# Up projection of a gated feed-forward layer: eight pairs of column tiles computed as seven block products, in an interleaved order

## The chip, the cores and the metric

The kernel runs on one core of a Trainium2 chip. The metric is the device time of one execution in microseconds, the median of several runs; smaller is better. Inputs are laid out by the host (slices, transposes, stacks), and everything that is arithmetic runs on the chip.

## The reference, cut to what matters

One layer of a hybrid trunk for 512 tokens with 1024 channels, in float32. A convolution branch and a linear-attention branch are merged and added to x, giving `h`; then comes the feed-forward part that the change is in (F = 2816):

```python
u2 = _rmsnorm(h, norm2_g[l])
z = _causal_dwconv(u2 @ w_ffn_up[l], ffn_dw_w[l], ffn_dw_b[l])
h = h + (jax.nn.silu(z[..., :FFN_DIM]) * z[..., FFN_DIM:]) @ w_ffn_down[l]
return _rmsnorm(h, final_g)
```

The up projection has 5632 columns, of which column c and column 2816 + c form one product (value and gate). The convolution runs over time, is causal, 3 wide, and separate for each column.

## The kernel before, in words

**Precision.** Each float32 operand is held as a sum of two numbers in a shorter format, hi and lo, and each product is three matmuls (`mm3`, L306 to L311: lo x hi, hi x lo, hi x hi). Of a weight block the hi part is a cast on ScalarE and the lo part a subtraction on VectorE (`split_weight`, L266 and L267; for the blocks of the down projection L239 and L240).

**Weights.** A list `order` names every weight block in the order of its use. `load` lets SyncE's queue (SP) fetch the next block, 128 x 1024 numbers or 512 KB, into a ring of 4 raw places; `split_weight` splits the next one and calls `load`; `weight` hands out a split block after `prefetch` has had the next LOOK = 2 split. So a load's place in SP's queue follows from the split before it, and a load waits until the last reader of its raw place is done. Each engine runs its instructions in the order in which the program issues them.

**The up projection.** A column tile is 128 of the 5632 columns for all 512 tokens, in one PSUM bank. `col_tile` (L313) goes over the 8 blocks of 128 channels, 3 matmuls of 128 x 512 each: 24. There are FT = 22 value tiles i and 22 gate tiles FT + i. On a finished tile `ffn_conv` (L1099) runs the convolution: a ScalarE operation with the bias (L1102) and two VectorE operations (L1104), both reading PSUM. `glu` applies silu to the value tile (L1110) and multiplies it by the gate tile (L1112).

**Pairs and groups.** The 22 products are taken in pairs (p, q), eleven in all, and the pairs in GROUPS of 4, 3 and 4. `first_of_pair` and `second_of_pair` (L1121, L1129) form sums and differences of the halves of 256 tokens and split them into hi and lo (`fsplit`, L1116 to L1118). After a group's pairs, `seven("w_down", ...)` (L972) multiplies them by the rows of the down projection and adds into `hres` (L1023). It computes each 2 x 2 block product (two halves of tokens, the two members of a pair) by seven block products in place of eight, named a11, a12, s1, n2, s4, n3, a22, from sums of the activations and sums of the weights. GpSimd's DMA queue adds weight blocks up while loading (L208, L225). The same function did the projection `w_o` before.

**The order around the change.** Group 0's first pair is done in a loop of its own (L1212 to L1218): its first three tiles go by halves of 256 tokens, since the last tokens are not normalized yet. From then on each pair is four whole tiles in the order p, FT + p, q, FT + q, then first and second of pair; at the end of a group the down projection follows, and then the next group's first tile. The working tiles `w`, `f`, `v` have two buffers each, `kept` (summed down-projection weights) two, `tmp` five; PSUM has five `mm` and three `ax` banks.

## Time and profile before

| what | value |
|---|---|
| median of 3 runs | 837.06 us (836.98 to 837.22) |
| the profiled execution | 838.15 us |
| its span in the trace | 836.5 us |
| granted TensorE clock | 0.998 |
| feed-forward part in the trace | about 482 to 836.5 us |
| HBM read, written | 95.03 MB, 2.10 MB |

The profiled execution is one run by itself; the span is the time between its first and last instruction in the trace. All rows shown from the trace are of this execution. PE is TensorE's matmul, PEld its weight load, DVE VectorE, ACT ScalarE, POOL GpSimd, SP SyncE. A row like `wlo<-raw,whi 128x1024 fp32r<-128x1024 f32 x42 | 50.9, 1216 | 3.5` means: output and inputs by the program's names, shape and type, 42 of them, 50.9 us busy together, 1216 ns each on average, 3.5 us idle of that engine just before them. A window row gives for each engine the busy time and in brackets the number of instructions in it. Matmuls overlap one another, so their durations do not add up; the distance of their starts does.

### The profile page before, as it was taken

Reading aid. Unit: us, or ns where it says so; the run is one execution under the profiler, and the core shown is the slowest. Engines: PE = TensorE matmul, PEld = TensorE weight load, DVE = VectorE, ACT = ScalarE, POOL = GpSimd, SP = SyncE. Lnnn points to the kernel's source line nnn. Section 1 sums busy time; section 2 is a strip of 40 time slices with the busy share of each in tenths; the row PEclk is TensorE's granted clock in tenths of the full one; section 3 lists DMA queues with packets and bytes.
Section 4 is the critical chain, followed back from the end, with each engine's and each line's share of the span. In section 5 each row is a group of like instructions: output and inputs, shape, how many; then the busy total and the mean of one; then the engine's idle time right before and its main releaser. Section 6 shows DMA issues by size and latency. Waiting matters only on the chain.

```text
span 836.5 us, 9981 instructions
## 1 busy us (share of the span) xinstructions
PE 827.9 (99%) x3821; PEld 692.4 (83%) x3821; DVE 651.6 (78%) x927; ACT 392.0 (47%) x544; POOL 43.1 (5%) x65
## 2 busy tenths in 40 slices
PE   9999999999999999999999999999999999999996
PEld 8888888888888888888888898888888888888885
DVE  5689879999998798744688858778757687677795
ACT  6723337537533422449435554444434444444454
POOL 1000000000001100000001000001000010000111
PEclk9999999999999999999999999999999999999999
DMA  8233222222322322222348643234742249222462
GB/s 313 99 103 101 85 100 88 93 98 76 101 76 76 126 92 88 98 100 77 102 100 229 194 157 108 94 97 105 214 151 88 66 88 284 101 87 93 101 125 102
DMA packets 28305, 97.79 MB, mean 117 GB/s; under 512 B 3208, under 2 KB 3344, under 8 KB 28256
## 3 DMA queue, kind: packets, MB, share of 16 engines
q1 hardware_dynamic: 24800, 85.35, 29.8%
q0 software_dynamic: 3456, 11.80, 8.3%
q8 instruction: 30, 0.49, 0.2%
q14 instruction: 19, 0.16, 0.1%
HBM read 95.03 MB, written 2.10 MB: 116 GB/s over the span
## 4 chain that ended last, share of the span: by engine, by line
PE 97%; DVE 1%; DMA 0%; issue 0%; ACT 0%; POOL 0%; POOLq 0%; SPq 0%; ACTq 0%
PE mm L309 29%; PE mm L311 29%; PE mm L310 29%; PE mm L521 3%; PE ax L862 1%; PE ax L309 1%; PE ax L311 1%; PE ax L310 1%; PE ax L435 1%; PE ax L864 1%; PE ax L844 1%; PE ax L831 0%; DVE hres L1023 0%; DMA x<-in_x_dram 0%; PE ax L830 0%; PE ax L388 0%
## 5 line engine op out<-in xcount | busy, mean ns | idle before, releaser
L309 PE MATMUL mm<-uh,wlo 128*128 128x512 f32 (+1 forms) x760 | 293.0, 385 | 0.0
L311 PE MATMUL mm<-uh,whi 128*128 128x512 f32 (+1 forms) x760 | 290.8, 383 | 0.0
L310 PE MATMUL mm<-ul,whi 128*128 128x512 f32 (+1 forms) x760 | 290.6, 382 | 0.0
L266 ACT CAST whi<-raw 128x1024 fp32r<-128x1024 f32 x114 | 118.8, 1046 | 124.3 <-PE mm L311 92.4
L267 DVE TENSOR_TENSOR wlo<-raw,whi 128x1024 fp32r<-128x1024 f32 x114 | 138.4, 1218 | 36.1 <-ACT whi L266 35.9
L311 PEld LDWEIGHTS mm<-uh,whi 128*128 128x128 f32 x760 | 142.8, 188 | 28.0
L310 PEld LDWEIGHTS mm<-ul,whi 128*128 128x128 f32 x760 | 142.9, 188 | 27.8
L309 PEld LDWEIGHTS mm<-uh,wlo 128*128 128x128 f32 x760 | 142.9, 188 | 27.2
L615 DVE SCALAR_TENSOR_TENSOR c<-h,pp,c 128x511 f32<-128x511 f32 (+14 forms) x240 | 162.4, 727 | 0.7
L1104 DVE SCALAR_TENSOR_TENSOR tmp<-mm,pp,tmp 128x511 f32<-128x511 f32 x88 | 65.9, 749 | 68.7 <-ACT tmp L1102 67.5
L1102 ACT ACTIVATE tmp<-mm,pp 128x512 f32<-128x512 f32 x44 | 34.3, 780 | 61.8 <-PE mm L311 61.8
L239 ACT CAST whi<-kept 128x1024 fp32r<-128x1024 f32 (+1 forms) x32 | 31.7, 995 | 23.1 <-PE mm L311 14.4
L240 DVE TENSOR_TENSOR wlo<-kept,whi 128x1024 fp32r<-128x1024 f32 (+1 forms) x32 | 36.6, 1152 | 3.0 <-ACT whi L239 2.8
L1023 DVE TENSOR_TENSOR hres<-hres,mm 128x512 f32<-128x512 f32 (+1 forms) x49 | 32.7, 671 | 3.4 <-PE mm L311 2.8
L239 ACT CAST whi<-raw 128x1024 fp32r<-128x1024 f32 (+1 forms) x24 | 23.7, 995 | 19.1 <-PE mm L311 19.0
L240 DVE TENSOR_TENSOR wlo<-raw,whi 128x1024 fp32r<-128x1024 f32 (+1 forms) x24 | 27.3, 1152 | 3.4 <-ACT whi L239 3.3
L310 PE MATMUL mm<-wlo,sh 128*128 128x512 f32 x66 | 25.8, 391 | 0.0
L311 PE MATMUL mm<-whi,sh 128*128 128x512 f32 x66 | 25.7, 390 | 0.0
L309 PE MATMUL mm<-whi,sl 128*128 128x512 f32 x66 | 25.5, 389 | 0.0
L309 PE MATMUL mm<-h,wlo 128*128 128x512 f32 x64 | 25.0, 391 | 0.0
L310 PE MATMUL mm<-h,whi 128*128 128x512 f32 x64 | 24.9, 389 | 0.0
L311 PE MATMUL mm<-h,whi 128*128 128x512 f32 x64 | 24.9, 389 | 0.0
(258 smaller groups left out, 1131.6 us busy)
## 6 DMA issues: line engine op xcount, KB each, us to landing
raw<-in_w_up_dram SPq DMA_DIRECT2D x44, 512.0 KB, 3.4
raw<-in_w_glu_dram SPq DMA_DIRECT2D x16, 512.0 KB, 3.4
raw<-in_w_down_dram SPq DMA_DIRECT2D x15, 512.0 KB, 3.3
kept<-in_w_down_dram POOLq DMA_DIRECT2D x10, 512.0 KB, 5.4
raw<-in_w_v_dram SPq DMA_DIRECT2D x8, 512.0 KB, 3.9
raw<-in_w_qk_dram SPq DMA_DIRECT2D x8, 512.0 KB, 3.2
raw<-in_w_r_dram SPq DMA_DIRECT2D x8, 512.0 KB, 3.3
raw<-in_w_gb_dram SPq DMA_DIRECT2D x8, 512.0 KB, 3.2
```

Of the source, the lines that this page charges most:

```text
L239: nc.scalar.copy(hi, raw)
L240: nc.vector.tensor_tensor(lo, raw, hi.bitcast(F32), ALU.subtract)
L266: nc.scalar.copy(hi, raw)
L267: pace[0] = nc.vector.tensor_tensor(lo, raw, hi.bitcast(F32), ALU.subtract)
L309: nc.tensor.matmul(acc, ll, rh, start=first, stop=False, **kw)
L310: nc.tensor.matmul(acc, lh, rl, start=False, stop=False, **kw)
L311: nc.tensor.matmul(acc, lh, rh, start=False, stop=last, **kw)
L521: nc.tensor.matmul(acc, act, ready[k // 2][wi][:, j], start=first, stop=last)
L615: nc.vector.scalar_tensor_tensor(y[:, s:], c[:, : T - s], w, y[:, s:], ALU.mult, ALU.add)
L1023: nc.vector.tensor_tensor(hres[t, n][:, c], hres[t, n][:, c], acc[:, c], op)
L1102: nc.scalar.activation(z, acc, AF.Identity, bias=pp[:, PP_FB + m : PP_FB + m + 1], scale=w[2])
L1104: nc.vector.scalar_tensor_tensor(z[:, s:], acc[:, : T - s], w[j], z[:, s:], ALU.mult, ALU.add)
```

## The change

In 8 of the 11 pairs (two of group 0, three of group 1, three of group 2) the second member q is computed as one 2 x 2 block product: two halves of 256 tokens by the two column tiles q and FT + q, over two halves of 512 channels. `up_pair` does it by seven block products of 4 channel blocks, 3 matmuls each, 256 tokens wide: 84 matmuls of 128 x 256 in place of 48 of 128 x 512.

- **Weights.** The two raw blocks and a third raw place for sums form four parts, x1, x3, x2, x4, split in this order (1024, 1024, 1024 and 512 columns). `up_sums` adds the blocks' halves on GpSimd: three additions of 128 x 512 after the split of x1, one after the split of x3.
- **Activations.** `sum_acts` forms, once, in group 0, the four sums s1, n2, s4, n3 of the halves of `u2` (10 VectorE operations of 128 x 1024) and splits them into hi and lo. They lie in buffers that were free or are shared (`kept`, `x`, `gain`, `btmp`, `us`).
- **Results.** The products are put together in two working tiles c1, c2: 4 copies from PSUM on ScalarE and 3 VectorE operations of 256 columns, and the convolution of q's tiles reads these. It read PSUM before.
- **Order.** `up_plan` writes the sequence. A unit is one seven-product pair and the two plain tiles of the next first member f, cut at k blocks and interleaved with the parts. So plain tiles run one place ahead; the last unit of a group computes the first member of the next group ahead of the down projection ("closes"), and the first unit of the groups opens differently ("opens").
- **Refill.** `refill` replaces the single `load` after each split: 4 raw entries ahead of the splits, and 2 in the up projection from group 0's seven-product part on.
- **Small moves.** `att` and `gate_up` lie in another pool; the load of `final_g` moves from the start of the feed-forward part to just before the last down projection; the down projection's loads are kept in program order; `w`, `f` and `v` have one buffer each; silu, gate and product are separate functions.

The core of the diff, first the order, the weights and the tiles (a line of "..." marks what is left out):

```diff
+        pairs = GROUPS[gi]
+        whole = range(KT)
+        def halves(*cuts):
+            return [range(a, b) for a, b in zip((0, *cuts), (*cuts, KT))]
+        def unit(q, f, kind):
+            a, b = f, FT + f
+            x1, x3, x2, x4 = (("part", q, part) for part in ("x1", "x3", "x2", "x4"))
+            a1, a2 = (("tile", a, ks) for ks in halves(4))
+            if kind == "opens":
+                b1, b2, b3 = (("tile", b, ks) for ks in halves(4, 6))
+                seq = [a1, x1, a2, x3, b1, x2, b2, x4, ("second", q), b3]
+            elif kind == "closes":
+                a1, a2, a3 = (("tile", a, ks) for ks in halves(3, 6))
+                seq = [x1, a1, x3, a2, x2, a3, x4, ("second", q), ("tile", b, whole)]
+            else:
+                b1, b2 = (("tile", b, ks) for ks in halves(4))
+                seq = [x1, a1, x3, a2, x2, b1, x4, ("second", q), b2]
+            return seq + [("first", f)]
+        firsts = [p for p, _ in pairs[1:]]
+        if gi + 1 < len(GROUPS):
+            firsts.append(GROUPS[gi + 1][0][0])
+        plan = []
+        n = 0
+        if gi == 0:
+            (p, q), (f, _) = pairs[1:3]
+            for i, role in ((p, "first"), (q, "second"), (f, "first")):
+                plan += [("tile", i, whole), ("tile", FT + i, whole), (role, i)]
+            n = 2
+        while n < len(firsts):
+            last = n + 1 == len(firsts) and gi + 1 < len(GROUPS)
+            kind = "closes" if last else "opens" if n == 0 else ""
+            plan += unit(pairs[n][1], firsts[n], kind)
+            n += 1
+        if n < len(pairs):
+            q = pairs[n][1]
+            plan += [("tile", q, whole), ("tile", FT + q, whole), ("second", q)]
+        return plan
+    def up_order(plan):
+        out = []
+        for what, i, *rest in plan:
+            if what == "part":
+                out.append(("w_up7", (i, rest[0])))
+            if what == "tile" and 0 in rest[0]:
+                out.append(("w_up", i))
+        return out
     order = [("w_v", j) for j in range(KT // 2)]
...
@@ -157,9 +211,13 @@
     order += [("w_conv", m) for pair in O_PAIRS for m in pair]
     order += [("w_o", (O_PAIRS, step, d)) for step, d in STEPS]
     for gi, pairs in enumerate(GROUPS):
-        order += [("w_up", j) for pair in pairs for i in pair for j in (i, FT + i)]
+        if gi == 0:
+            order += [("w_up", j) for i in pairs[0] for j in (i, FT + i)]
+            first7 = len(order) + 6
+        order += up_order(up_plan(gi))
         order += [("w_down", (pairs, step, d)) for step, d in STEPS]
     ready, raws = [], []
+    pair_raws = {}
     kept = {}
     used = [0]
...
                 return
+            if name == "w_up7":
+                q, part = j
+                if part == "x1":
+                    pair_raws[q] = [raw_tile() for _ in range(2)]
+                    for raw, m in zip(pair_raws[q], (q, FT + q)):
+                        nc.sync.dma_start(raw, a["w_up"][m])
+                raws.append(None)
+                return
             raw = raw_tile()
             nc.sync.dma_start(raw, a[name][j])
             raws.append(raw)
+    def refill():
+        while len(raws) < len(order):
+            few = len(raws) >= first7 and order[len(raws)][0] != "w_down"
+            if len(raws) >= len(ready) + (2 if few else 4):
+                return
+            load()
     def raw_tile():
...
             dst = raw_tile()[:, :n]
-        nc.sync.dma_start(dst, src)
+        load_dma = nc.sync.dma_start(dst, src)
+        if name == "w_down":
+            tc.keep_in_program_order(load_dma)
         if step == "n3":
             nc.gpsimd.dma_start(dst, block(name, pairs, d, 1, 1), accum_op=ALU.add)
...
+    def up_operand(q, part):
+        raws = pair_raws[q]
+        return {"x1": lambda: raws[0], "x3": lambda: raws[2], "x2": lambda: raws[1], "x4": lambda: raws[2][:, :T]}[part]()
+    def up_sums(q, part):
+        add = lambda out, x, y: nc.gpsimd.tensor_tensor(out, x, y, ALU.add)
+        left, right = slice(0, T), slice(T, D)
+        if part == "x1":
+            one, two = pair_raws[q]
+            three = raw_tile()
+            pair_raws[q].append(three)
+            add(three[:, left], one[:, left], two[:, left])
+            add(three[:, right], three[:, left], two[:, right])
+            add(two[:, left], two[:, left], two[:, right])
+        if part == "x3":
+            one, _, three = pair_raws[q]
+            add(three[:, left], three[:, right], one[:, right])
     def split_weight(halves=False, between=None):
...
@@ -310,11 +406,11 @@
         nc.tensor.matmul(acc, lh, rl, start=False, stop=False, **kw)
         nc.tensor.matmul(acc, lh, rh, start=False, stop=last, **kw)
-    def col_tile(w, acts, acc=None, lo=0, hi=T, at={}):
+    def col_tile(w, acts, acc=None, lo=0, hi=T, at={}, ks=range(KT)):
         if acc is None:
             acc = mm_bank()
-        for k in range(KT):
+        for k in ks:
             s = slice(k * P, (k + 1) * P)
...
@@ -1094,7 +1190,6 @@
     conv_scope.close()
     heap_scope.close()
     ffn_scope, fp = scoped("ffn", 1)
-    gain3 = load_gain("final_g")
     def ffn_conv(acc, m):
```

and the sums, the products and the loop (of `sum_acts`, the chains and the places):

```diff
         y = fsplit(v, 3 * H, "s")
         acts["s1"], acts["n2"], acts["s4"] = y(0), y(1), y(2)
         return acts
+    seven_acts = {}
+    def sum_acts():
+        def f32(x):
+            return x.bitcast(F32)
+        def part(t, k):
+            return [u2[k][j][:, :, t * H : (t + 1) * H] for j in range(2)]
+        a11, a12, a21, a22 = part(0, 0), part(0, 1), part(1, 0), part(1, 1)
+        def tile(pool, tag, bufs, k=4):
+            return pool.tile([P, k, H], F32R, tag=tag, name=nm(tag + "s"), bufs=bufs)
+        def chain(engine, out, start, *terms):
+            for op, x in terms:
+                engine.tensor_tensor(out, start if start.dtype == F32 else f32(start), f32(x), op)
+                start = out
+            return out
+        def split_sum(src, his, lo):
+            n = 4 // len(his)
+            for j, hi in enumerate(his):
+                ks = slice(j * n, (j + 1) * n)
+                nc.scalar.copy(hi, src[:, ks])
+                nc.vector.tensor_tensor(lo[:, ks], src[:, ks], f32(hi), ALU.subtract)
+            return [hi[:, k, :] for hi in his for k in range(n)], [lo[:, k, :] for k in range(4)]
+        add, sub = ALU.add, ALU.subtract
+        lo = {"n3": tile(fp, "us", 3), "s1": tile(fp, "us", 3), "n2": tile(fp, "us", 3), "s4": tile(tp, "x", 3)}
+        hi = {"n3": [tile(tp, "btmp", 2, 2) for _ in range(2)], "s1": [tile(tp, "x", 3)]}
+        hi |= {"n2": [tile(tp, "x", 3)], "s4": [tile(tp, "gain", 1)]}
+        def room(_):
+            return keep_tile("w_down").rearrange("p (k t) -> p k t", k=4)
+        src = {step: room(step) for step in ("s1", "n2")}
+        chain(nc.vector, src["s1"], a21[0], (sub, a22[0]), (add, a21[1]), (sub, a22[1]))
+        chain(nc.vector, src["n2"], src["s1"], (sub, a11[0]), (sub, a11[1]))
+        yield
+        for step in ("n2", "s1"):
+            seven_acts[step] = split_sum(src[step], hi[step], lo[step])
+        yield
+        src |= {step: room(step) for step in ("s4", "n3")}
+        chain(nc.vector, src["s4"], src["n2"], (add, a12[0]), (add, a12[1]))
+        chain(nc.vector, src["n3"], a11[0], (sub, a21[0]), (add, a11[1]), (sub, a21[1]))
+        yield
+        for step in ("n3", "s4"):
+            seven_acts[step] = split_sum(src[step], hi[step], lo[step])
+        for step, x in (("a11", a11), ("a12", a12), ("a22", a22)):
+            seven_acts[step] = [[y[:, k, :] for k in range(4)] for y in x]
+        yield
+    def up_step(acc, step, w, half, opens):
+        ah, al = seven_acts[step]
+        for k in range(4):
+            s = slice(half * T + k * P, half * T + (k + 1) * P)
+            mm3(acc[:, :H], (w[0][:, s], w[1][:, s]), (ah[k], al[k]), opens and k == 0, k == 3, not opens)
+    def up_pair(q):
+        x, y, z = mm_bank(), ax_bank(), ax_bank()
+        c1, c2 = tmp(), tmp()
+        t1, t2 = slice(0, H), slice(H, T)
+        def put(c, acc):
+            nc.scalar.copy(c, acc[:, :H])
+        def combine(c, l, r, op):
+            nc.vector.tensor_tensor(c, l, r, op)
+        w = weight("w_up7", (q, "x1"))
+        up_step(x, "a11", w, 0, True)
+        put(c1[:, t1], x)
+        up_step(z, "a12", w, 1, True)
+        combine(c1[:, t1], c1[:, t1], z[:, :H], ALU.add)
+        yield
+        w = weight("w_up7", (q, "x3"))
+        up_step(x, "n2", w, 1, False)
+        put(c2[:, t1], x)
+        up_step(y, "s1", w, 0, True)
+        put(c2[:, t2], y)
+        yield
+        w = weight("w_up7", (q, "x2"))
+        up_step(x, "n3", w, 0, False)
+        combine(c2[:, t2], c2[:, t2], x[:, :H], ALU.subtract)
+        up_step(y, "s4", w, 1, False)
+        combine(c2[:, t1], y[:, :H], c2[:, t1], ALU.subtract)
+        yield
+        up_step(x, "a22", weight("w_up7", (q, "x4")), 0, False)
+        put(c1[:, t2], x)
+        yield [c1, c2]
...
@@ -1204,9 +1402,10 @@
             for t in range(2):
                 ends[t].store()
+    gain3 = None
+    banks, values, units = {}, {}, {}
     for gi, pairs in enumerate(GROUPS):
         acts = []
...
-
-        def both(i):
-            return early.get(i) or [col_tile(weight("w_up", i), acts2), col_tile(weight("w_up", FT + i), acts2)]
-
-        for p, q in pairs:
-            w, found = first_of_pair(p, both(p))
-            acts.append(second_of_pair(q, both(q), w, found))
+            p, q = pairs[0]
+            w = first_gated(p, value(p, accs[0]), accs[1])
+            found = first_of_pair(w)
+            sums = sum_acts()
+            next(sums)
+            acts.append(second_of_pair(q, value(q, accs[2]), accs[3], w, found))
+            next(sums)
+        else:
+            found = first_of_pair(w)
+        for what, i, *rest in up_plan(gi):
+            if what == "tile":
+                if 0 in rest[0]:
+                    banks[i] = (weight("w_up", i), mm_bank())
+                wt, acc = banks[i]
+                col_tile(wt, acts2, acc, ks=rest[0])
+                if KT - 1 in rest[0] and i < FT:
+                    values[i] = value(i, acc)
+            if what == "part":
+                if rest[0] == "x1":
+                    units[i] = up_pair(i)
+                done = next(units[i])
+                if done:
+                    values[i] = value(i, done[0])
+                    banks[FT + i] = (None, done[1])
+            if what == "first":
+                w = first_gated(i, values.pop(i), banks.pop(FT + i)[1])
+                if any(i in pair for pair in pairs):
+                    found = first_of_pair(w)
+            if what == "second":
+                acts.append(second_of_pair(i, values.pop(i), banks.pop(FT + i)[1], w, found))
+            if gi == 0 and len(acts) < 3 and what != "tile" and sums:
+                sums = None if next(sums, 1) else sums
         if gi < len(GROUPS) - 1:
             seven("w_down", pairs, acts, lambda t, n, c: None)
```

More of the change, by code (lines that the diff above doesn't have):

```diff
@@ L123, in trunk_layer @@
     pp = cp.tile([P, PP_N], F32, name="pp")
-    gate_up = cp.tile([P, HEADS * DK], F32R, name="gate_up")
+    gate_up = gp.tile([P, HEADS * DK], F32R, name="gate_up")
     ones = cp.tile([P, P], F32, name="ones")
@@ L129, in trunk_layer @@
     keep = cp.tile([P, P], U8, name="keep")
-    att = cp.tile([P, NT, P], F32, name="att")
+    att = gp.tile([P, NT, P], F32, name="att")
     def load_consts():
@@ L144, in load_consts, with up_plan @@
         nc.gpsimd.memset(att, 0.0)
+    def up_plan(gi):
+        pairs = GROUPS[gi]
[43 more added lines that the diff above has]
+        return out
     order = [("w_v", j) for j in range(KT // 2)]
@@ L233, in split_weight @@
             name, spec = order[len(ready)]
-            if name in SEVEN:
-                raw = operand(raw, *spec)
+            if name in SEVEN or name == "w_up7":
+                raw = operand(raw, *spec) if name in SEVEN else up_operand(*spec)
                 n = raw.shape[-1]
@@ L240, in split_weight @@
                 nc.vector.tensor_tensor(lo, raw, hi.bitcast(F32), ALU.subtract)
-                sum_on(name, *spec)
+                sum_on(name, *spec) if name in SEVEN else up_sums(*spec)
                 ready.append((hi, lo))
-                load()
+                refill()
                 return
@@ L251, in split_weight @@
                 ready.append((hi, None))
-                load()
+                refill()
                 return
@@ L268, in split_weight @@
             ready.append((hi, lo))
-            load()
+            refill()
     def prefetch(n):
@@ L1105, in ffn_conv, with value, gated @@
         return z
-    def glu(i, accs, out):
-        za = ffn_conv(accs[0], i)
+    def value(i, acc):
+        za = ffn_conv(acc, i)
         nc.scalar.activation(za, za, AF.Silu)
-        zb = ffn_conv(accs[1], FT + i)
+        return za
+    def gated(i, za, acc, out):
+        zb = ffn_conv(acc, FT + i)
         nc.vector.tensor_tensor(out, za, zb, ALU.mult)
@@ L1205, in last_at @@
                 ends[t].store()
+    gain3 = None
+    banks, values, units = {}, {}, {}
     for gi, pairs in enumerate(GROUPS):
         acts = []
-        early = {}
         if gi == 0:
@@ L1229, in trunk_layer @@
         else:
+            gain3 = load_gain("final_g")
             seven("w_down", pairs, acts, last_complete, last_at, True)
```

19 lines of the change are left out of this document (10 added, 9 removed).

## The prediction

> **What bounds the kernel now.** I read the page first, then busy time by stage, then TensorE's own timeline in the stage that changes.
>
> ```profile
> span 836.5 us, 9981 instructions
> PE 827.9 (99%) x3821; PEld 692.4 (83%) x3821; DVE 651.6 (78%) x927; ACT 392.0 (47%) x544; POOL 43.1 (5%) x65
> ...
> PE 97%; DVE 1%; DMA 0%; issue 0%; ACT 0%; POOL 0%; POOLq 0%; SPq 0%; ACTq 0%
> ```
>
> TensorE is busy 99% of the span and 97% of the chain of waits is its own work: a stage ends when its matmuls end. Less matmul time is less time, as long as the other engines deliver. The next view cuts the feed-forward part into stages: the halved tiles, group 0's up projection, its down projection, and group 2's up projection. The columns are busy time and instruction count of TensorE, weight load, VectorE, ScalarE and GpSimd, then granted clock, DMA share and GB/s.
>
> ```profile
> core 0: us, PE busy (x) PEld busy (x) DVE busy (x) ACT busy (x) POOL busy (x), PEclk, DMA share, GB/s
> 482.00:501.00 19.00, 19.00 (x161) 18.99 (x160) 11.32 (x16) 8.73 (x13) 1.37 (x1) 1.00 0.47 155
> 501.00:571.80 70.80, 70.80 (x315) 58.62 (x314) 52.56 (x72) 33.63 (x44) 1.75 (x2) 1.00 0.36 103
> 571.80:609.90 38.10, 38.10 (x170) 31.55 (x169) 30.13 (x37) 16.50 (x17) 3.46 (x4) 1.00 0.66 175
> ...
> 704.00:788.50 84.50, 84.50 (x374) 69.97 (x373) 58.24 (x78) 38.52 (x50) 1.74 (x2) 1.00 0.37 108
> ```
>
> TensorE has no gap there and the clock is full, so nothing hides a change of its work. VectorE is second: 52.56 of 70.80 us, 74%. GpSimd does almost nothing, 1.75 us.
>
> **The change part by part: TensorE.** One row of TensorE's timeline is start, duration, operation; matmuls overlap, so the spacing of the starts is what counts.
>
> ```profile
> 495.28 0.28 PE L309 MATMUL mm<-uh,wlo 128*128 128x256 f32 x1
> ...
> 501.04 0.40 PE L309 MATMUL mm<-uh,wlo 128*128 128x512 f32 x1
> ...
> 506.51 0.39 PE L309 MATMUL mm<-uh,wlo 128*128 128x512 f32 x1
> ...
> 566.35 0.39 PE L309 MATMUL mm<-uh,wlo 128*128 128x512 f32 x1
> ```
>
> From 495.28 to 501.04 stand two tiles by halves, 48 matmuls of 256 columns: 5.76/48 = 0.1200 us each. From 506.51 to 566.35 stand eleven whole tiles, 264 matmuls of 512 columns: 59.84/264 = 0.2267. Two tiles before: 48 x 0.2267 = 10.88. The seven block products of 4 k-blocks and 3 matmuls: 84 x 0.1200 = 10.08. One pair gains 0.80, eight gain **6.4 us**. By the count of columns alone it would be an eighth of 10.88, 1.36 a pair and 10.9 in all; the narrow matmul costs 0.0067 more than half of the wide one, and this takes 4.5 of it back. The plain tiles, cut into pieces of their k loop, keep their matmuls and only change places.
>
> **VectorE, the engine that must keep up.** Rows below are a group's count, busy time, mean ns of one, idle time before.
>
> ```profile
> L267 DVE TENSOR_TENSOR wlo<-raw,whi 128x1024 fp32r<-128x1024 f32 x42 | 50.9, 1216 | 3.5 <-ACT whi L266 3.5
> L1104 DVE SCALAR_TENSOR_TENSOR tmp<-mm,pp,tmp 128x511 f32<-128x511 f32 x44 | 33.0, 750 | 67.5 <-ACT tmp L1102 67.5
> L1104 DVE SCALAR_TENSOR_TENSOR tmp<-mm,pp,tmp 128x510 f32<-128x510 f32 x44 | 32.9, 747 | 1.2
> L1118 DVE TENSOR_TENSOR sl<-v,sh 128x768 fp32r<-128x768 f32 x11 | 10.5, 956 | 0.0
> L1118 DVE TENSOR_TENSOR yl<-w,yh 128x512 fp32r<-128x512 f32 x11 | 7.6, 692 | 6.9 <-ACT yh L1117 6.9
> L1112 DVE TENSOR_TENSOR w<-tmp,tmp 128x512 f32<-128x512 f32 x11 | 7.5, 685 | 0.0
> L1118 DVE TENSOR_TENSOR al<-f,ah 128x512 fp32r<-128x512 f32 x11 | 7.5, 684 | 0.0
> L1125 DVE TENSOR_TENSOR w<-w 128x256 f32<-128x256 f32 x11 | 4.7, 424 | 0.3
> L1023 DVE TENSOR_TENSOR hres<-hres,mm 128x256 f32<-128x256 f32 x2 | 0.8, 419 | 0.0
> L240 DVE TENSOR_TENSOR wlo<-raw,whi 128x512 fp32r<-128x512 f32 x3 | 2.0, 683 | 0.0
> ```
>
> A unit of the new plan is a plain column pair and a seven-product pair: four tiles. Before, VectorE did for it 4 splits (4.86), 8 convolution steps (5.99), 2 products (1.37), first-of-pair work 0.424 + 0.692, second-of-pair work 3 x 0.424 + 0.684 + 0.956: 16.2 us in 22 instructions. After there are 5 splits of 1024 and one of 512 (6.08 + 0.68), and 3 combines of 256 out of PSUM, priced by the L1023 row, 3 x 0.419: 19.4 us in 26 instructions. Successive ones overlap a little:
>
> ```profile
> 501.99 1.22 DVE L267 TENSOR_TENSOR wlo<-raw,whi 128x1024 fp32r<-128x1024 f32 x1
> 503.12 0.68 DVE L1112 TENSOR_TENSOR w<-tmp,tmp 128x512 f32<-128x512 f32 x1
> ```
>
> The second starts 0.09 before the first ends; with 0.08 for each of 26, VectorE needs 17.3 us of a unit that TensorE leaves in 10.88 + 10.08 = 20.96 us: 83%. The 67.5 us idle before the 44 first convolution steps are waits for a tile that TensorE had not finished, not lost work. So VectorE fits, with 3.6 us of room a unit where it had 7.3 of 21.76.
>
> **ScalarE.** A seven-product pair adds two and a half weight casts less two, and 4 copies of 256:
>
> ```profile
> L266 ACT CAST whi<-raw 128x1024 fp32r<-128x1024 f32 x114 | 118.8, 1046 | 124.3 <-PE mm L311 92.4 <-issue 31.5 <-PE mm L521 0.2
> L1102 ACT ACTIVATE tmp<-mm,pp 128x512 f32<-128x512 f32 x44 | 34.3, 780 | 61.8 <-PE mm L311 61.8
> ...
> L867 ACT ACTIVATE junk<-ax 128x256 bf16<-128x256 f32 x16 | 6.1, 384 | 2.7 <-PE ax L864 2.5
> ```
>
> 3.5 casts in place of 2 are 1.5 x 1.05 = 1.6 us, 4 copies at 0.384 are 1.5: 3.1 more on an engine that was 33.63 of 70.80 busy (10.3 of 21.76). 13.4 of 20.96 is 64%: hidden.
>
> **The sums of activations, group 0 only.** VectorE gets 10 sums of 128x1024 and the low parts of four splits. From the end of the last activation split,
>
> ```profile
> 491.68 1.29 DVE L393 TENSOR_TENSOR ul<-ax,uh 128x512 fp32r<-128x512 f32 x2 [1.37 <-ACT uh L392]
> ```
>
> at 492.97, the order of the changed program has 41 VectorE instructions up to the weight split of the fifth whole tile after 506.51: the 10 sums, 2 low parts and 5 weight splits (17 x 1.216), 12 convolution steps (9.0), and 7.2 for products, differences and splits. That is 36.9 less 41 x 0.08 = 33.6, and one wait for ScalarE of 0.6: done at 527.2. TensorE wants it at 506.51 + 4 x 5.44 = 528.3. This is the tightest place, 1.1 us of room. A sum is unlike a split only in adding; that row, 1.216, is its price from both sides, and 10% more on the twelve would be 1.5, 0.4 late.
>
> **GpSimd's four adds of 128x512 a pair.** The trace has no such add. Below: the one row of 128x512 on GpSimd, a memset, 0.524; above: three such streams, two read and one written, 1.57.
>
> ```profile
> L144 POOL MEMSET att<- 128x512 f32 x1 | 0.5, 524 | 0.0
> ```
>
> I take two streams, 1.05. Four of them, 4.2 in 20.96 us, fit an empty engine. They stand between the split of x1 and that of x3. Part x1 and half a column tile lie between the uses of the two, 24 x 0.1200 + 12 x 0.2267 = 5.6 us, so the three adds that x3 needs, 3.2, cost nothing by their length alone. (The Trainium skill, "GPSIMD Engine Reference", § 3.1, gives 4497 ns for a tensor_tensor of 2048 elements; an estimate by its quarter, 1.1, would leave the sum as it is. No run here shows it.)
>
> **Weights, buffers, queues.** A pair still loads two blocks of 512 KB, so no transfer is added.
>
> ```profile
> raw<-in_w_up_dram SPq DMA_DIRECT2D x44, 512.0 KB, 3.4
> ```
>
> The raw ring keeps 4 places, and a pair holds a third one for its sums, so a plain tile's load waits for the split that frees a place: 3.4 landing, 1.05 cast, 1.22 split, 5.7 us, inside the 10 us that two parts last. The new refill rule puts one more weight load ahead of the last piece of x in SP's queue at the start:
>
> ```profile
> 12.52 0.38 SPq L406 DMA_DIRECT2D x<-in_x_dram  x1
> 15.04 0.33 SPq L174 DMA_DIRECT2D raw<-in_w_glu_dram  x1
> ```
>
> ```profile
> 21.45 1.05 ACT L455 ACTIVATE junk<-x 128x1024 bf16<-128x1024 f32 x1
> ```
>
> That load waits for a raw place until 15.04, so x leaves at some 15.4 in place of 12.52, and lands 3.4 later, at 18.8 (with half as much again for the crowd at the start, 20.5), ahead of its first use at 21.45: cover of 1 to 2.6 us. The last gain's load, moved behind the earlier down-projection loads, is needed only at the end, and the single buffers of w, f, v are freed by the same VectorE that fills them again. For the places where in-order engines wait for each other (eight units, two of them opening and two closing a group, and the start) I charge **1 us** in all: my choice, between 0 and the 5 us at which a unit would lose its 3.6 of room in part. What is late next if the up projection shrinks is VectorE, not DMA (share 0.36).
>
> **The sum.** -6.4 + 1.0 = -5.4 us. The profiled execution took 838.15 us with a span of 836.5, 1.65 outside it; the sum is made on the span and gives 832.75 for such an execution. The median of the runs shown is 837.06, 1.1 below; so **831.7 us**.
>
> **The rivals.**
>
> **1. GpSimd's adds hold VectorE (slower).** The rows that bear on it:
>
> ```profile
> 468.35 0.57 POOL L359 TENSOR_TENSOR rstd<-var,mhalf 128x1 f32<-128x1 f32 x1 [10.15 <-DVE var L1061]
> 472.31 1.41 POOL L359 TENSOR_TENSOR rstd<-var,mhalf 128x1 f32<-128x1 f32 x1 [3.39 <-DVE var L1061]
> 481.30 0.55 POOL L359 TENSOR_TENSOR rstd<-var,mhalf 128x1 f32<-128x1 f32 x1 [7.58 <-DVE var L1061]
> 485.27 1.37 POOL L359 TENSOR_TENSOR rstd<-var,mhalf 128x1 f32<-128x1 f32 x1 [3.42 <-DVE var L1061]
> ```
>
> ```profile
> 472.09 1.22 DVE L240 TENSOR_TENSOR wlo<-kept,whi 128x1024 fp32r<-128x1024 f32 x1
> ...
> 485.01 1.22 DVE L267 TENSOR_TENSOR wlo<-raw,whi 128x1024 fp32r<-128x1024 f32 x1
> ```
>
> A GpSimd operation of one element takes 0.55, but 1.41 and 1.37 when a VectorE split of 1.22 had started 0.2 before it: it ends 0.4 after the split does. So the two exclude each other, and GpSimd waits. The other direction, VectorE behind a long GpSimd add, no row shows. If it holds, each add costs VectorE its whole length, except where VectorE works out of PSUM: per unit the 4 plain convolution steps (3.0) and 3 combines (1.26), 4.3 of 19.4, 22%. Unit: 17.3 + 0.78 x 4.2 = 20.6, and two waits for ScalarE's first convolution step (L1102), 0.78 each, that VectorE then has no room to absorb: 22.1 against 20.96. Eight units lose 1.2 each, 9.4, less 6.4: +3.0, **840.1**. It decides from a unit of 21.76: adds of 0.93 and up; with 0.524 the unit is 20.5 and the forecast stands, with 1.57 it is 23.8 and the time 853. For it: one direction is in the rows, VectorE is at 83%. Against it: the adds run in a stretch where VectorE waits for TensorE anyway. (The Trainium skill, "SBUF — State Buffer", section "Who interferes with whom", says that a VectorE instruction with two SBUF inputs and a GpSimd instruction that reads SBUF hold each other off, whoever came first keeping the port for its whole instruction. By that rule, this rival; the rows agree for the one direction.) Chance 0.24.
>
> **2. The feed is late in part (smaller gain).** The single spare raw place, the 1.1 us at group 0's sums or the closing units give 2 to 4 us back: 833.5 to 835.4. For it: room of 1 to 3 us a unit in an in-order chain. Against: 17% idle. Chance 0.10.
>
> **3. The seven products don't shorten the work (no change).** If matmuls of 256 in the new order, with the weight changing after each and banks changing each twelve, ran at 0.1295 (10.88/84), nothing would be gained. Against it: 0.1200 over 48 with a new weight each time; for it, only that these stand beside each other in one tile. With other losses of 5 us together, chance 0.08: 835.4 to 838.7.
>
> **How the numbers follow.** A measurement of this kernel can tell about 0.2%, 1.7 us. Forecast 0.58 (830.3, where no unit waits, to 833.5), rival 2 0.10, rival 3 0.08, rival 1 0.24. Faster: 0.58 + 0.10 = 0.68; same 0.08; slower 0.24. The range reaches from 830.3 to 842, past rival 1's price and leaving out its upper half, some 0.11, and 0.03 below: 0.86 held. It is wide since both signs lie in it; the likeliest case's own is 830.3 to 833.5.
>
> **What would show it.** Right: matmuls of 256 at 0.120 apart in the up projection, no idle TensorE of over 0.3 us in the units, VectorE at some 83% there, splits of 1.22, GpSimd adds near 1.05. Wrong: idle TensorE before a seven-product part, released by VectorE's wlo (rival 2, or 1 if splits or sums lengthen beside GpSimd's adds, or GpSimd's adds last over 2 us); 256-wide matmuls 0.13 apart (rival 3); a last piece of x after 21.45, which shifts everything behind it.

## The result, and the profile after

| | changed kernel | kernel before |
|---|---|---|
| median of 6 runs | 833.92 us (832.77 to 835.00) | 837.14 us (836.36 to 838.15) |
| profiled execution | 833.95 us | 838.15 us |
| span in the trace | 832.2 us | 836.5 us |

The ratio is 0.9959, 95% interval 0.9946 to 0.9971: faster by 0.3 to 0.5%, 3.2 us by the medians. 831.7 was forecast, 5.4 us less. 833.92 lies in the range given, 830.3 to 842, but not in the likeliest case's own, 830.3 to 833.5. The profiled execution of before is at the upper end of its runs, so the two traces stand 4.3 us apart and the medians 3.2; the interval holds both, and the readings below are of the traces.

The head of the page after, against the lines of before:

```profile
span 832.2 us, 10782 instructions
PE 822.1 (99%) x4109; PEld 699.8 (84%) x4109; DVE 697.7 (84%) x982; ACT 417.7 (50%) x597; POOL 98.1 (12%) x97
...
PE 86%; DVE 5%; DMA 4%; issue 2%; ACT 1%; POOL 0%; SPq 0%; POOLq 0%; ACTq 0%; DVEq 0%
```

TensorE lost 5.8 us of busy time. VectorE gained 46, GpSimd 55. The chain of waits was 97% TensorE and is 86% now. That share is a loose measure: 20 us of the chain's DMA time lie at 442 to 470, ahead of the changed part, and two more profiles of the same kernel give 92%. The same windows as before show more (columns as there; the changed kernel runs up to 4 us ahead in the later ones):

```profile
501.00:571.80 70.80, 70.80 (x383) 61.51 (x382) 67.09 (x87) 40.74 (x58) 12.49 (x8) 1.00 0.33 105
...
609.90:675.20 65.30, 64.83 (x397) 57.57 (x396) 51.86 (x66) 34.19 (x49) 20.51 (x12) 1.00 0.30 99
...
704.00:788.50 84.50, 84.15 (x489) 74.37 (x488) 70.42 (x95) 48.56 (x69) 23.50 (x14) 1.00 0.45 142
```

The second of these windows (group 1's up projection) in the kernel before:

```profile
609.90:675.20 65.30, 65.30 (x290) 54.07 (x289) 42.88 (x57) 27.89 (x36) 1.71 (x2) 1.00 0.31 92
```

In group 0, VectorE is busy 67.09 of 70.80 us (52.56 before) and TensorE has no gap. In the two later groups it has gaps of half a microsecond where it had none. TensorE's waits over the whole span (what it waited for, us in total, times, longest):

```profile
...
PE mm L405 <- ACT tmp L1315: 0.7, 2, 0.4
...
```

That line is the copy `put` of a bank, and it is the only wait of the feed-forward part that is long enough to be listed. The whole account of the part: from its first narrow matmul to its last one it took 482.01 to 829.12 before and 481.96 to 824.86 after, 347.11 and 342.90, 4.2 us less. Of the 6.4 forecast for the products, the rest went to two things.

First, the **switch of widths**. A run of 12 wide matmuls between two runs of narrow ones:

```profile
541.97 0.40 PE L405 MATMUL mm<-uh,wlo 128*128 128x512 f32 x1
...
544.72 0.28 PE L405 MATMUL mm<-xs,wlo 128*128 128x256 f32 x1
```

That is 2.75 us where 12 x 0.2267 is 2.72. Some thirty runs of wide matmuls between narrow ones show an excess of 0.02 to 0.03 each, about 0.7 us in all; the narrow runs keep their 0.1200.

Second, **four gaps**, at 616.5, 646.4, 667.4 and 738.8, 0.38 + 0.61 + 0.1 + 0.61 = 1.7 us with the slower matmul after each. So -6.4 + 0.7 + 1.7 = -4.0, against -4.2 measured; the other 0.2 is a short delay at 688 that the trace of before has and this one doesn't. The gap at 616.5 is short to tell: on VectorE a weight split beside GpSimd's adds takes 2.31 in place of 1.22, and the hres addition behind it frees a bank at 616.78 that TensorE takes at 616.83.

```profile
613.86 2.31 DVE L363 TENSOR_TENSOR wlo<-raw,whi 128x1024 fp32r<-128x1024 f32 x1
616.10 0.68 DVE L1119 TENSOR_TENSOR hres<-hres,mm 128x512 f32<-128x512 f32 x1
```

The gap at 646.4 is read from three engines. TensorE:

```profile
646.13 0.39 PE L407 MATMUL mm<-uh,whi 128*128 128x512 f32 x1
646.87 0.38 PE L405 MATMUL mm<-xs,wlo 128*128 128x256 f32 x1 [0.35 <-ACT tmp L1315]
```

ScalarE ahead of it:

```profile
643.81 1.06 ACT L362 CAST whi<-raw 128x1024 fp32r<-128x1024 f32 x1 [0.58 <-PE ax L407]
645.25 0.63 ACT L1204 ACTIVATE tmp<-tmp 128x512 f32<-128x512 f32 x1 [0.39 <-DVE tmp L1199]
645.79 0.76 ACT L1197 ACTIVATE tmp<-mm,pp 128x512 f32<-128x512 f32 x1
646.46 0.36 ACT L1315 COPY tmp<-mm 128x256 f32<-128x256 f32 x1
```

VectorE ahead of that:

```profile
642.05 3.77 DVE L1199 SCALAR_TENSOR_TENSOR tmp<-tmp,pp,tmp 128x511 f32<-128x511 f32 x4
```

of which the second step by itself is

```profile
642.71 1.79 DVE L1199 SCALAR_TENSOR_TENSOR tmp<-tmp,pp,tmp 128x511 f32<-128x511 f32 x1
```

and GpSimd, beside it:

```profile
642.21 1.75 POOL L310 TENSOR_TENSOR raw<-raw,raw 128x512 f32<-128x512 f32 x1 [6.76 <-DVE wlo L336]
```

Read it from the last to the first. GpSimd's fourth add of a pair runs from 642.21 to 643.96. VectorE has four convolution steps there, which now read SBUF. The one that starts beside the add, at 642.71, takes 1.79 us and ends 0.5 behind the add; the other three take 0.74 to 0.75. So the silu (L1204) waits, the copy out of the bank of a11 stands behind it in ScalarE's queue, and n2 can't be added into that bank until 646.8. At 667.4 and 738.8 the same step is held by the same add.

How much of VectorE is held shows in its groups, 482 to 832 us: those with both inputs in SBUF are longer on average, those that read PSUM are not.

```profile
L336 DVE TENSOR_TENSOR wlo<-raw,whi 128x1024 fp32r<-128x1024 f32 x39 | 50.4, 1296 | 14.7 <-ACT whi L335 11.0 <-PE mm L407 3.7
L363 DVE TENSOR_TENSOR wlo<-raw,whi 128x1024 fp32r<-128x1024 f32 x26 | 35.8, 1378 | 3.0 <-ACT whi L362 3.0
...
L1199 DVE SCALAR_TENSOR_TENSOR tmp<-mm,pp,tmp 128x511 f32<-128x511 f32 x28 | 20.8, 742 | 4.6 <-ACT tmp L1197 4.5
...
L1199 DVE SCALAR_TENSOR_TENSOR tmp<-tmp,pp,tmp 128x511 f32<-128x511 f32 x16 | 16.5, 1070 | 0.1
```

GpSimd's adds themselves:

```profile
L310 POOL TENSOR_TENSOR raw<-raw,raw 128x512 f32<-128x512 f32 x24 | 38.3, 1597 | 144.6 <-DVE wlo L336 65.4 <-DVE wlo L363 42.4 <-DMA raw<-in_w_up_dram 36.2
L310 POOL TENSOR_TENSOR raw<-raw 128x512 f32<-128x512 f32 x8 | 16.8, 2094 | 0.0
```

1.05 was the estimate and 1.57 its upper end; the 32 adds take 55.1 us together, 1.72 each.

### The profile page after: what moved, and what is told of

Its sections match the earlier page's. It is cut to its first block, busy times and chain, and to the rows that moved or that the text cites. A ratio compares the mean times of both kernels' runs of the same rounds, so it can differ in the third digit from the quotient of the medians.

```text
span 832.2 us, 10782 instructions
## 1 busy us (share of the span) xinstructions
PE 822.1 (99%) x4109; PEld 699.8 (84%) x4109; DVE 697.7 (84%) x982; ACT 417.7 (50%) x597; POOL 98.1 (12%) x97
## 4 chain that ended last, share of the span: by engine, by line
PE 86%; DVE 5%; DMA 4%; issue 2%; ACT 1%; POOL 0%; SPq 0%; POOLq 0%; ACTq 0%; DVEq 0%
PE mm L405 24%; PE mm L406 24%; PE mm L407 24%; PE mm L617 3%; PE ax L405 2%; PE ax L407 2%; PE ax L406 2%; DMA kept<-in_w_o_dram 2%; DVE tmp L1199 1%; DVE wlo L336 1%; DMA raw<-in_w_down_dram 1%; DMA hres<-in_x_dram 1%; PE ax L958 1%; DVE hres L1119 1%; PE ax L960 1%
## 5 line engine op out<-in xcount | busy, mean ns | idle before, releaser
L405 PE MATMUL mm<-uh,wlo 128*128 128x512 f32 (+1 forms) x696 | 261.6, 376 | 0.0
L406 PE MATMUL mm<-ul,whi 128*128 128x512 f32 (+1 forms) x696 | 259.3, 373 | 0.0
L407 PE MATMUL mm<-uh,whi 128*128 128x512 f32 (+1 forms) x696 | 259.0, 372 | 0.0
L362 ACT CAST whi<-raw 128x1024 fp32r<-128x1024 f32 x98 | 102.5, 1048 | 126.3 <-PE mm L407 82.2
L363 DVE TENSOR_TENSOR wlo<-raw,whi 128x1024 fp32r<-128x1024 f32 x98 | 123.3, 1261 | 35.6 <-ACT whi L362 35.4
L336 DVE TENSOR_TENSOR wlo<-raw,whi 128x1024 fp32r<-128x1024 f32 (+1 forms) x56 | 65.0, 1167 | 16.5 <-ACT whi L335 12.6
L335 ACT CAST whi<-raw 128x1024 fp32r<-128x1024 f32 (+1 forms) x56 | 53.8, 964 | 28.2 <-PE mm L407 21.3
L310 POOL TENSOR_TENSOR raw<-raw,raw 128x512 f32<-128x512 f32 x24 | 38.3, 1597 | 144.6 <-DVE wlo L336 65.4
L1199 DVE SCALAR_TENSOR_TENSOR tmp<-mm,pp,tmp 128x511 f32<-128x511 f32 (+1 forms) x56 | 41.3, 740 | 4.6 <-ACT tmp L1197 4.5
L1197 ACT ACTIVATE tmp<-mm,pp 128x512 f32<-128x512 f32 x28 | 21.7, 775 | 20.5 <-PE mm L407 20.4
L1199 DVE SCALAR_TENSOR_TENSOR tmp<-tmp,pp,tmp 128x511 f32<-128x511 f32 (+1 forms) x32 | 27.1, 904 | 0.1
```

Source lines behind the costliest of these rows:

```text
L310: add = lambda out, x, y: nc.gpsimd.tensor_tensor(out, x, y, ALU.add)
L335: nc.scalar.copy(hi, raw)
L336: nc.vector.tensor_tensor(lo, raw, hi.bitcast(F32), ALU.subtract)
L362: nc.scalar.copy(hi, raw)
L363: pace[0] = nc.vector.tensor_tensor(lo, raw, hi.bitcast(F32), ALU.subtract)
L405: nc.tensor.matmul(acc, ll, rh, start=first, stop=False, **kw)
```

## The experiments

Theory A: the products save 6.4, the switches cost 0.7, and the rest is lost where GpSimd's adds hold VectorE. Theory B: the rest is lost to the in-order chain of splits, copies and banks, whatever GpSimd does. Rival C: the new order, and not the products, makes the difference. Each group of runs shared a chip and the runs of before; medians of before were 836.73, 836.73 and 836.68 us.

**The changed kernel again.** No edit; the measure for the first group.

> The changed kernel once more, on the chip of the other three, to measure them against. Theory A (seven products save TensorE 6.4 us, 0.8 goes to some thirty switches between wide and narrow matmuls, 1.5 to stalls that begin at GpSimd's adds holding VectorE) and theory B (the stalls come from the in-order chain of splits, copies and banks, whatever GpSimd does): both 0.995 to 0.997 of the kernel before, some 833 to 834.5 us.

834.18 us (833.13 to 834.92), ratio 0.9967 (0.9955 to 0.9978). In the third group it was run as `after_once_more`:

> The changed kernel, beside the next two on one chip: 833 to 834.5 us, 0.995 to 0.997 of the kernel before.

833.45 us, ratio 0.9965 (0.9952 to 0.9977). Three sets agree on 2.5 to 3.2 us.

**The adds left out.**

```diff
-            three = raw_tile()
+            three = two
             pair_raws[q].append(three)
-            add(three[:, left], one[:, left], two[:, left])
-            add(three[:, right], three[:, left], two[:, right])
-            add(two[:, left], two[:, left], two[:, right])
...
-            add(three[:, left], three[:, right], one[:, right])
```

> GpSimd's four adds a pair are left out, so the parts x3, x2, x4 are the raw gate block and the up projection's values are not the reference's; the third raw place goes with them. Theory A: VectorE's splits and convolution steps are all back at their own lengths (1.22 and 0.74, where they average 1.30 to 1.38 and 1.07 now), the four stalls of 0.3 to 0.6 us of TensorE go, 1.3 us less than the changed kernel with its adds. Theory B: the stalls stay, within 0.4 us of it.

831.62 us (830.86 to 832.34), ratio 0.9938 (0.9926 to 0.9950): 2.6 us below the changed kernel, 5.1 below the kernel before. The groups of VectorE in the same window are back at their own lengths:

```profile
L333 DVE TENSOR_TENSOR wlo<-raw,whi 128x1024 fp32r<-128x1024 f32 x39 | 47.4, 1221 | 17.3 <-ACT whi L332 13.6 <-PE mm L404 3.7
L360 DVE TENSOR_TENSOR wlo<-raw,whi 128x1024 fp32r<-128x1024 f32 x26 | 31.7, 1221 | 3.8 <-ACT whi L359 3.8
...
L1196 DVE SCALAR_TENSOR_TENSOR tmp<-mm,pp,tmp 128x511 f32<-128x511 f32 x28 | 20.9, 747 | 5.4 <-ACT tmp L1194 5.3
...
L1196 DVE SCALAR_TENSOR_TENSOR tmp<-tmp,pp,tmp 128x511 f32<-128x511 f32 x16 | 11.4, 746 | 0.1
```

No wait of TensorE is left in the feed-forward part, with the same order of instructions on VectorE and ScalarE. VectorE was busy 303.9 us from 482 to 832 in the changed kernel of this group and 287.6 here: the adds held it 16.3 us in all, 2.0 a pair. Not all of the 2.6 is theirs: from the first narrow matmul of the feed-forward part to its last, the two traces take 343.3 us with the adds and 341.3 without, 1.9 less, and the rest of their distance lies ahead of that part, where nothing was changed. So theory A holds, with 1.9 for the 1.3 that was expected from the gaps. Two things went with the adds: the third raw place, so that a little may be earlier loads, and the wait of ScalarE's casts for the sums. The latter is small in the changed kernel's trace, 2.7 and 1.1 us in one pair (712 to 718), and TensorE has no gap behind it.

**The adds on VectorE.**

```diff
-        add = lambda out, x, y: nc.gpsimd.tensor_tensor(out, x, y, ALU.add)
+        add = lambda out, x, y: nc.vector.tensor_tensor(out, x, y, ALU.add)
```

> The same adds on VectorE, 0.68 each, 2.7 us a pair, queued in order behind the split of x1. Theory A: VectorE gives up 2.7 a unit and gets back the 1.9 by which it was held; it has room for the rest, the stalls go in part: 0.3 to 1.3 us less than the changed kernel. Theory B: 0.8 a unit more on an in-order engine lengthens the chain: 0.5 to 3 us more. If VectorE waits for a pair's weights to land, with its other work queued behind, it is more than that.

835.69 us (834.71 to 839.18, 12 runs), ratio 0.9992 (0.9981 to 1.0003): 1.5 us above the changed kernel; of its gain of 2.6, 1.0 is left by the medians, and the interval of the ratio reaches past 1. VectorE isn't held now (its splits take 1.22), but it waits, in its queue, for the weights of a pair to land:

```profile
L310 DVE TENSOR_TENSOR raw<-raw,raw 128x512 f32<-128x512 f32 x24 | 16.5, 687 | 5.3 <-DMA raw<-in_w_up_dram 5.2
```

and what stands behind it are the hres additions that free the banks of the down projection:

```profile
PE mm L405 <- DVE hres L1119: 2.7, 3, 1.5
```

Theory A's 0.3 to 1.3 less didn't come. The time is in theory B's range, 0.5 to 3 more, but what the trace shows is the wait for weights that the last sentence of the expectation named. GpSimd's holds are the cheaper of the two here: in the changed kernel its adds wait 36.2 us for the same loads (their row further up), and nothing that TensorE is short of stands behind them.

**The order alone.** The parts of a pair are plain halves of its two tiles; no sums, no narrow matmuls beyond the old ones.

```diff
-        w = weight("w_up7", (q, "x1"))
-        up_step(x, "a11", w, 0, True)
...
+        for j, part in enumerate(("x1", "x2")):
+            w = weight("w_up7", (q, part))
+            out.append(mm_bank())
+            col_tile(w, acts2, out[j], ks=range(4))
+            yield
+            col_tile(w, acts2, out[j], ks=range(4, KT))
```

> The new order with no seven products: the four parts of a pair are the four halves (in k) of its two plain tiles, with no sums of weights or activations. Theory A: the order itself moves nothing, TensorE has its old matmuls: the time of the kernel before within 0.5 us. A rival C, that the order (plain tiles ahead across the ends of groups) has a part in the gain, gives 1 us or more below the kernel before; if the order costs, 1 us or more above.

836.26 us (835.48 to 837.82), ratio 0.9996 (0.9988 to 1.0005): the time of before. Rival C falls.

**The narrow matmul by itself.** In the kernel before, the 16 tiles go by two halves of 256 tokens.

```diff
+            for j in (i, FT + i):
+                wt, acc = weight("w_up", j), mm_bank()
+                for lo in (0, H):
+                    col_tile(wt, acts2, acc, lo, lo + H)
```

> The kernel before with the 16 column tiles of the eight pairs as two halves of 256 tokens each, in the old order: the price of the width by itself. By the spacings 0.1200 and 0.2267 a pair of tiles costs 96 x 0.1200 - 48 x 0.2267 = 0.64 more, eight 5.1 us: 842 us. If the narrow matmul cost nothing beyond its columns, 837.

841.93 us (841.78 to 843.02), 5.2 above before, where 5.1 was worked out. The price of the narrow matmul, and so the 6.4, stands.

**Steps swapped.**

```diff
-        up_step(x, "n2", w, 1, False)
-        put(c2[:, t1], x)
         up_step(y, "s1", w, 0, True)
         put(c2[:, t2], y)
+        up_step(x, "n2", w, 1, False)
+        put(c2[:, t1], x)
```

and the same for s4 ahead of n3.

> Within a pair s1 is multiplied ahead of n2, and s4 ahead of n3, so that the copy that empties the bank of a11 (and that of s1) has 12 narrow matmuls, 1.44 us, more before the bank is written again. The adds stay on GpSimd. Theory A1: TensorE's waits for that copy (two of 0.35, with 0.2 to 0.3 around each) are one end of the hold, they go, and the rest stays: 0.6 to 1.2 us less than the changed kernel. Theory A2: the copy is late by the hold of the whole chain and the wait shows up again at the next weight split: no difference within 0.4.

832.09 us (831.83 to 834.27), ratio 0.9948 (0.9935 to 0.9960). Once more, beside the changed kernel:

> The kernel with s1 ahead of n2 and s4 ahead of n3 once more, to see whether its gain over the changed kernel holds on one chip: if the two waits for the copy were worth what the trace shows, 0.6 to 1.2 us less than the changed kernel; if the 832.09 was partly chance, that is what is left of the 1.9 seen.

833.10 us (831.81 to 833.44), ratio 0.9955 (0.9942 to 0.9967), against 833.45. In both traces the waits for the copy are gone, as A1 says. A part of A2 came too: both have a new delay at 676, 0.4 us with the slower matmul behind it, where TensorE waits for VectorE's combine of n3, which now stands last; the first of the two also waits 0.7 at 708.9 for a weight cast. The gain by medians is 2.1 and 0.4 us; from the first narrow matmul of the part to the last, the traces take 343.3 and 342.6 us, where the three of the changed kernel take 342.9, 343.3 and 343.5. So the size of the gain is not settled, and the 2.1 is not in the part that was changed. Both traces keep the wait for the hres addition at 617, 0.5 us, late behind a split that the first pair's adds hold.

**The swap with the adds of five pairs on VectorE.**

```diff
+        engine = nc.gpsimd if any(q == g[0][1] for g in GROUPS) or q == GROUPS[0][2][1] else nc.vector
+        add = lambda out, x, y: engine.tensor_tensor(out, x, y, ALU.add)
```

> The same swap, and the adds of five pairs on VectorE; those of the first pair with seven products of each group stay on GpSimd (with them on VectorE it waited 5.2 us for weights to land, with hres adds behind, and TensorE lost 1.46, 0.83 and 0.42 us there). Theory A: the holds go in five pairs and the waits of the three others don't come; only the hold at the start of group 1 stays, 0.3 to 0.7: 1 to 2 us less than the changed kernel, 832 to 833. Theory B (in order, VectorE has no room for 2.7 us a pair): no better than the adds all on VectorE less the three waits, 833 to 834.5.

833.54 us (832.90 to 834.35), ratio 0.9963 (0.9950 to 0.9977): no better than the swap, and within the changed kernel's own runs. 833.54 is in theory B's range and the interval reaches into A's, so it tells little; it is no version to take. Its trace still has the hres wait of 0.5 at 616.

**The adds doubled.**

```diff
             add(three[:, left], one[:, left], two[:, left])
-            add(three[:, right], three[:, left], two[:, right])
+            add(three[:, left], one[:, left], two[:, left])
+            for _ in range(3):
+                add(three[:, right], three[:, left], two[:, right])
```

(and the fourth add twice.)

> Each pair issues eight adds on GpSimd in place of four, repeats of adds with the same result. If the price is what VectorE is held (2.0 us a pair with four adds, against about 3.3 of room), eight hold it 4 us, over its room: stalls of 1 us a pair and up, and the three adds that x3 waits for are now six, some 10 us against 5.6 of cover, so up to 4 us more a pair: 842 to 870 us. If the holds only cost by chance places, 834 to 837.

873.78 us (872.67 to 874.26), ratio 1.0439: beyond the expected range. VectorE was held only 9.7 us more in all (313.5 busy), so its room is not what 40 us went to. ScalarE, in one pair:

```profile
761.60 1.05 ACT L338 CAST whi<-raw 128x1024 fp32r<-128x1024 f32 x1 [6.14 <-POOL raw L310]
...
769.20 0.36 ACT L1318 COPY tmp<-mm 128x256 f32<-128x256 f32 x1
```

The cast of x3 waits for six adds, 752.09 to 761.57, and the copies and convolutions behind it in ScalarE's queue wait with it; TensorE waited five times for such a copy, 26.4 us in all, 7.5 at the longest. The length of the chain ahead of x3 is a second price of the adds. With three adds ahead of x3 it lies under its cover, with six it doesn't.

Some 8 of the 40 us are not waits. Behind six of the waits TensorE's narrow matmuls stand 0.213 apart in place of 0.120, for 2.6 to 3.8 us each. The granted clock is 0.50 in such a stretch (columns as in the windows above, the clock third from the end):

```profile
770.00:773.00 3.00, 3.00 (x16) 3.00 (x16) 3.00 (x7) 0.99 (x2) 0.00 (x0) 0.50 0.50 175
```

**Four idle adds a pair.** To separate holding from chain length, adds that nobody waits for.

```diff
             add(three[:, left], three[:, right], one[:, right])
+            for _ in range(4):
+                add(idle, idle, idle)
```

> Behind each pair's fourth add GpSimd does four more of 128x512 on a tile that nobody reads: eight adds that contend for VectorE, but only four that anything waits for. Theory H (in the kernel with doubled adds the price was VectorE held over its room): VectorE is held some 2 us a pair more, and with 17.3 + 4 of 20.96 it has no room: TensorE stalls 0.5 to 2 us a pair, 838 to 850 us. Theory L (it was the length of the chain of six adds ahead of x3): little happens, 834 to 836.5, and VectorE's operations lengthen all the same.

849.71 us (848.44 to 850.55), ratio 1.0151 (1.0135 to 1.0166). The time is in theory H's range, but by another road: nothing holds these adds back, so all 32 were put ahead, into group 0.

```profile
489.90 45.26 POOL L310 TENSOR_TENSOR idle<-idle 128x512 f32<-128x512 f32 x28
```

There they show the hold by itself. VectorE's groups from 482 to 535 us, while the adds run:

```profile
L1267 DVE TENSOR_TENSOR kept<-kept,ul 128x1024 f32<-128x1024 f32 x4 | 7.1, 1787 | 0.1
L1201 DVE SCALAR_TENSOR_TENSOR tmp<-mm,pp,tmp 128x511 f32<-128x511 f32 x6 | 4.4, 736 | 0.0
...
L1212 DVE TENSOR_TENSOR w<-tmp,tmp 128x512 f32<-128x512 f32 x1 | 1.5, 1523 | 0.0
```

1.22 has become 1.79 and 0.69 became 1.52, with the steps out of PSUM at 0.736. TensorE waits 3.47 and 6.32 us for weight splits (L365) there, where the changed kernel has no gap. Behind the longer wait its wide matmuls stand 0.426 apart for 5 us, at a granted clock of 0.50, and that is 2.4 more. Another 2.7 come from the last tokens' normalization, whose GpSimd step stood in the queue behind the adds: from the first narrow matmul to the first whole tile it is 21.7 us, 19.0 in the changed kernel. A pair's adds spread over the units, as theory H wanted them, were not tried.

## Why the prediction was right, point by point

The sign and the wide range held, and the gain came from the term that was to bring it. The size was 3.2 us by the medians for 5.4, since the price of GpSimd's adds had been put at nothing. The range held rival 1's price too, so that 833.92 lies in it says little by itself; of the signs that were named for being right, no idle TensorE of over 0.3 us, splits of 1.22 and adds near 1.05 did not come.

- **TensorE's products, 6.4 us: right.** Narrow runs keep 0.1200 in the new order, and the width's price measured alone is 5.2 for 5.1. Rival 3 falls.
- **The order moves nothing: right** (836.26 against 836.73).
- **Group 0's sums, the tightest place: right.** The weight split for the fifth tile was to end at 527.2 and TensorE to want it at 528.3. Of the trace after:

```profile
525.86 1.22 DVE L363 TENSOR_TENSOR wlo<-raw,whi 128x1024 fp32r<-128x1024 f32 x1
```

it ends at 527.08, and TensorE starts that tile at 528.22 without a gap. GpSimd's first add starts at 529.00; the idle adds show what it costs when adds run there.

- **The last piece of x behind one more load: hidden, as costed.** It leaves at 15.51 (15.4 was forecast), lands at 20.21 (18.8 to 20.5) and is first used at 21.21.
- **GpSimd's adds "cost nothing by their length alone": the step that was mis-sized.** The term was 1.05 each and no hold in the sum; measured are 1.72 each and 2.0 us a pair of VectorE held. Rival 1's mechanism is therefore real, in the direction that no row of before showed, but its price was overrated: it lets each add cost VectorE 0.78 of its length, 3.3 us a pair, and two waits of 0.78 besides, 22.1 us a unit and 840.1. Measured are 2.0 of the adds' 6.9 us, 0.5 an add. An estimate from the forecast 17.3 and this 2.0 leaves the unit at 19.3 of 20.96. VectorE does not become the bound; some 1.9 us are lost at places where in-order queues touch, and that is rival 2's size (833.5 to 835.4, chance 0.10) by rival 1's cause.
- **The 1 us for waits: too little.** Gaps and switches took 2.4 in the trace; the switches, 0.7, stood in no term. With the adds away, the medians stand 5.1 us below before, and the feed-forward part is 5.8 shorter (341.3 for 347.1), for the 5.4 forecast.
- **Two slips that change nothing.** VectorE's list of a unit before has 21 instructions and not 22, and ScalarE gets three and a half casts less two, as the sum there has it.

The Trainium skill, "SBUF — State Buffer", section "Who interferes with whom", has the hold in both directions, between VectorE's instructions with two SBUF inputs and GpSimd's that read SBUF; a VectorE instruction with at most one SBUF input, outside the two-port modes, is not part of it. The traces agree: 1.22 became 1.79 beside the idle adds and 1.38 on average in the changed kernel, and the steps with one input in PSUM stayed at 0.74.

## What to carry to other kernels

An engine that is idle in the profile is not free: before giving it work, look whether its operations and those of the engine that has little room read SBUF at the same time, and whether the latter can read PSUM instead. An expected gain in TensorE is worked out from spacings of the very widths that will be used, and mixed widths get a small price for each switch. Where a bank is reused, the copy that empties it stands in an in-order queue behind unrelated work: put other matmuls between, and look what the swap makes late in its turn.

## What the runs showed of the hardware

- GpSimd's add of 128x512 took 1.29 us at the least in a pair, 1.72 on average beside a busy VectorE, and 1.04 at the least where one tile was both inputs (the idle adds); VectorE's takes 0.687.
- The hold is mutual and partial: 32 adds in a row (49.4 us) took up to 1.97 us each where the shortest took 1.04, and cost VectorE some 12 us (316.1 busy in the feed-forward part against 303.7 in the changed kernel on the same chip), and its operations out of PSUM nothing.
- A run of wide matmuls between narrow ones takes 0.02 to 0.03 us more than its spacings.
- Behind some waits of TensorE of 1.9 to 7.5 us its matmuls stood 1.8 to 1.9 times as far apart for 2.6 to 5 us, at a granted clock of 0.50; behind one of 3.47 they did not.
